# Gate and up tiles of three feed-forward layers from seven quarter products

## Chip, cores and metric

One core of a Trainium2 chip runs the whole program. The metric is device microseconds of one execution; the kernel before has a median of 2692.7 us over three runs (2689.73 to 2694.28). TensorE (PE) multiplies; VectorE (DVE), ScalarE (ACT) and GpSimd (POOL) do the rest, each taking its instructions in a fixed order; SyncE (SP) issues the DMAs. TensorE's clock has two levels, 1.2 and 2.4 GHz; the granted clock is given as a share of the upper one.

## The reference

Eight stages over a sequence of 512 positions with 1024 features: four mixers (two attentions, a state-space layer, a convolution), and after each a feed-forward layer of the same form:

```python
def swiglu_ffn(u, w_gate, w_up, w_down):       # u: 512 x 1024 (normed), F = 2816
    return (jax.nn.silu(u @ w_gate) * (u @ w_up)) @ w_down
x = x + swiglu_ffn(rmsnorm(x, g), w_gate, w_up, w_down)
```

All of it is fp32.

## The kernel before

Activations lie transposed: 8 chunks of 128 features x 512 positions. Each fp32 operand is split into two fp32r tiles, `hi` (a cast on ACT) and `lo` = value - `hi` (a subtraction on DVE; `split`, L293 and L294, for weights), and each product is three matmuls, hi x hi, hi x lo, lo x hi (`mm3`, L301 to L303), all accumulated in PSUM.

A feed-forward layer has 22 hidden tiles of 128 features. `gu` (L685) makes one tile j: it loads gate and up weights (two DMAs of 512 KB into the three `raw` buffers), splits them into the four `hi`/`lo` buffers of `wspl`, and runs 8 chunks x 2 x 3 = 48 matmuls of 512 columns, gate into PSUM tile `pg`, up into `pu`. Then silu(gate) x up goes into `s` (a name for the pool `z`, which has three buffers), and `hilo_of` splits it into a pair of `d` tiles. `dn` (L711) makes one of 8 output chunks from a range of hidden tiles and adds it to `xT` (L670, L674). The hidden tiles are taken in three parts (`PARTS`: 8, 7 and 7 tiles); after each part come 8 `dn` items over it.

Layers 0 and 1 come behind a `Split` norm, whose input h is already normed; their first `gu` takes tiles 0 and 1 together. Layers 2 and 3 come behind a `Norm`: h is only gained, and the row factor R (column sums on PE, an inverse square root of 13 small DVE instructions, a transpose on PE into `rb`, a copy on ACT) multiplies gate and up later (L704, L706). R is asked for once the first tile's matmuls are written.

The program is written tile by tile; a scheduler then fixes the order of each engine from its own timing of the program, and a buffer's next user waits until the last reader of it is done. `phase` opens the pools of a stage.

Of the kernel before, what the change touches and what calls it, by code (L numbers as in the profile page):

```python
# [10 lines left out]
F32 = mybir.dt.float32  # L11
F32R = mybir.dt.float32r
I32 = mybir.dt.int32
AF = mybir.ActivationFunctionType
OP = mybir.AluOpType
PSUM = bass.MemoryType.PSUM

T, NT, KC = 512, 4, 8
PARTS = ((0, 8), (8, 15), (15, 22))
F_HID, FC = 2816, 22  # L20
NEG = -1e30

# [66 lines left out]
def _layout(i):  # L89
# [20 lines left out]
    for n in range(4):  # L110
# [44 lines left out]
    "ssm": (SSB,  # L155
# [63 lines left out]
def _program(nc, tc, a, out, stages=STAGES):  # L219
    st = ExitStack()  # L220
    pool = lambda n, b, **k: st.enter_context(tc.tile_pool(name=n, bufs=b, **k))
    one = pool("one", 1)
    wraw = pool("wraw", 3)
# [3 lines left out]
    cur = {"sb": None, "ps": None}  # L227

    def phase(name, kinds=("sb", "ps")):
        for k in kinds:  # L230
            if cur[k]:
                cur[k][0].close()
            e = ExitStack()
            kw = {"space": PSUM} if k == "ps" else {}
            p = e.enter_context(tc.tile_pool(name=f"{k}_{name}", bufs=1, reuse_waits="tile", **kw))
            cur[k] = (e, p, PHASES[name][k == "ps"])

    def ptile(k, shape, dt, name):
        tag = ALIAS.get(name, name)
        _, p, bufs = cur[k]  # L240
        if k == "ps" and tag not in bufs:
            tag = {"tr": "pt", "st": "tr", "py": "tr"}[tag]
        return p.tile(shape, dt, tag=tag, name=name, bufs=bufs[tag])


    V, S, E, G = nc.vector, nc.scalar, nc.tensor, nc.gpsimd
# [27 lines left out]
    def tmp(name="t", dt=F32, n=T):  # L274
        return ptile("sb", [128, n], dt, name)
# [4 lines left out]
    def psum(name="ps"):  # L280
        return ptile("ps", [128, T], F32, name)

    last_load = [None]
# [6 lines left out]
    def split(raw, n, m=128, eng=None):  # L290
        hi = wspl.tile([128, n], F32R, tag="hi", name="hi")
        lo = wspl.tile([128, n], F32R, tag="lo", name="lo")
        S.copy(hi, raw)  # L293
        (eng or V).tensor_tensor(lo, raw, hi.bitcast(F32), op=OP.subtract)  # L294
        return hi.rearrange("p (k m) -> p k m", m=m), lo.rearrange("p (k m) -> p k m", m=m)

    def two(src):
        return [split(load(flat(src[:, i]), 1024), 1024) for i in range(2)]

    def mm3(ps, lh, ll, rh, rl, start, stop, **k):  # L300
        E.matmul(ps, lh, rh, start=start, stop=False, **k)  # L301
        E.matmul(ps, lh, rl, start=False, stop=False, **k)  # L302
        E.matmul(ps, ll, rh, start=False, stop=stop, **k)  # L303
# [7 lines left out]
    def flat(ap):  # L311
        return ap.rearrange("p k m -> p (k m)")
# [60 lines left out]
    def hilo_of(src, bias=None, gain=None, to="h"):  # L373
        if to == "h":
            hi, lo = (hp.tile([128, T], F32R, tag="h", name=n) for n in ("hi", "lo"))
        else:
            hi, lo = tmp(to, F32R), tmp(to, F32R)
        if gain is not None:
            S.activation(hi, src, AF.Copy, scale=gain)
            V.scalar_tensor_tensor(lo, src, gain, hi.bitcast(F32), op0=OP.mult, op1=OP.subtract)  # L380
        elif bias is not None:
            S.activation(hi, src, AF.Identity, bias=bias)
            V.scalar_tensor_tensor(lo, src, bias, hi.bitcast(F32), op0=OP.add, op1=OP.subtract)
        else:
            S.copy(hi, src)  # L385
            V.tensor_tensor(lo, src, hi.bitcast(F32), op=OP.subtract)
        return hi, lo
# [279 lines left out]
    def add_x(m, ps, gcol, bias=None, o=slice(0, T)):  # L667
# [5 lines left out]
        else:  # L673
            V.tensor_tensor(x, ps, x, op=OP.add)  # L674

    def ffn(n, nm, gcol, nxt):
        phase("ffn")
        direct = isinstance(nm, Split)
        h = nm.h
        d = {}  # L680

        def gu(js):
            def it():
                gr = []
                for j in js:  # L685
                    with tc.issue_after(nm.mark.ins) if direct and j == 1 else nullcontext():
                        W = direct and j == 0 and nm.W or two(a[f"w_gu{n}"][j])
                        gr += [(psum("pg"), W[0]), (psum("pu"), W[1])]
                if js[0] == 0 and direct:
                    nm.lin([gr[:2], gr[2:]])  # L690
                else:
                    lin(gr, h)
                if nm.R is None:
                    nm.finish().to_sbuf()
                R = nm.R
                for i, j in enumerate(js):
                    pg, pu = gr[2 * i][0], gr[2 * i + 1][0]
                    s = tmp("s")
                    if direct:
                        S.activation(s, pg, AF.Silu)  # L700
                        V.tensor_tensor(s, s, pu, op=OP.mult)
                    else:
                        u = tmp("su")
                        V.tensor_tensor(s, pg, R, op=OP.mult)  # L704
                        S.activation(s, s, AF.Silu)
                        V.tensor_tensor(u, pu, R, op=OP.mult)  # L706
                        V.tensor_tensor(s, s, u, op=OP.mult)
                    d[j] = hilo_of(s, to="d")
                return 10.4 * len(js), None
            return it  # L710

        def dn(m, lo, hi):
            def ev(ps):
                add_x(m, ps, gcol)
                return nxt.update(m) if nxt and hi == FC else None
            return item(a[f"w_dn{n}"][m][:, lo:hi], lambda: [d[j] for j in range(lo, hi)], ev, hi - lo)

        items = []
        for lo, hi in PARTS:
            if lo == 0 and direct:  # L720
                items += [gu([0, 1])] + [gu([j]) for j in range(2, hi)]
            else:
                items += [gu([j]) for j in range(lo, hi)]
            at = TAIL_AT["final" if isinstance(nxt, Final) else 7]
            n_tail = at[0] if hi == FC and isinstance(nxt, Split) else 0
            items += [dn(m, lo, hi) for m in range(KC - n_tail)]
            if n_tail:
                items.append(tail(range(KC - n_tail, KC), lambda m: a[f"w_dn{n}"][m][:, lo:hi], hi - lo,
                                  lambda: [d[j] for j in range(lo, hi)], gcol, nxt, ("pj",) * n_tail, at[1:]))
        return _stream(items)  # L730
# [939 lines left out]
    nm = None  # L1670
    if stages[0] != "mix0":
# [7 lines left out]
        nm = norms[stages[0]]().all()  # L1679
    for i, name in enumerate(stages):  # L1680
# [14 lines left out]
        else:  # L1695
            n = int(name[3])
            f = ffn(n, nm, (None, md0.col(40), md1.col(40))[n + 1] if n < 2 else None, nx)
# [5 lines left out]
        nm = nx  # L1703
# [19 lines left out]
```

## Time and profile before

| | |
|---|---|
| median of 3 runs | 2692.7 us |
| the profiled execution, its span | 2689.29 us, 2687.5 us |
| PE busy | 2554.3 us (95%) |
| DVE, ACT, POOL busy | 1611.3, 1056.1, 396.3 us |
| mean granted TensorE clock | 0.979 |

Busy time of PE counts any time in which a matmul is in flight, so PE at 100% says that it never waited, not that it ran at its peak. How long one matmul takes from the next is read from the start times in the timeline, not from durations, which overlap. In the timelines DVE instructions overlap too: a duration is longer than the distance to the next start.

### The profile page before, as it was taken

Reading aid. Unit: us, or ns where it says so; the run is one execution under the profiler, and the core shown is the slowest. Engines: PE = TensorE matmul, PEld = TensorE weight load, DVE = VectorE, ACT = ScalarE, POOL = GpSimd, SP = SyncE. Lnnn points to the kernel's source line nnn. Section 1 sums busy time; section 2 is a strip of 40 time slices with the busy share of each in tenths; the row PEclk is TensorE's granted clock in tenths of the full one; section 3 lists DMA queues with packets and bytes.
Section 4 is the critical chain, followed back from the end, with each engine's and each line's share of the span. In section 5 each row is a group of like instructions: output and inputs, shape, how many; then the busy total and the mean of one; then the engine's idle time right before and its main releaser. Section 6 shows DMA issues by size and latency. Waiting matters only on the chain.

```text
span 2687.5 us, 33768 instructions
## 1 busy us (share of the span) xinstructions
PE 2554.3 (95%) x13016; PEld 2155.4 (80%) x13016; DVE 1611.3 (60%) x2898; ACT 1056.1 (39%) x1881; POOL 396.3 (15%) x286
## 2 busy tenths in 40 slices
PE   5788989999999999999999999999999997999998
PEld 4666888888888888888788888788888877888887
DVE  8898765555457643333678786643444897543444
ACT  4457643222357542222455444422223554422222
POOL 3345120000113210000100000100001783100001
PEclk9988999999999999999999999999999997999999
DMA  7711135555421123333222122233323220332332
GB/s 270 230 53 40 32 101 198 176 174 187 144 81 32 48 88 101 91 97 95 87 79 72 55 79 59 91 104 100 94 94 95 64 63 16 100 103 95 94 97 69
DMA packets 81251, 265.40 MB, mean 99 GB/s; under 512 B 8897, under 2 KB 11329, under 8 KB 81089
## 3 DMA queue, kind: packets, MB, share of 16 engines
q1 hardware_dynamic: 81088, 263.24, 31.1%
q8 instruction: 102, 1.67, 0.3%
q14 instruction: 61, 0.49, 0.1%
HBM read 261.10 MB, written 2.10 MB: 98 GB/s over the span
## 4 chain that ended last, share of the span: by engine, by line
PE 79%; DVE 11%; POOL 3%; ACT 3%; issue 2%; DMA 2%; SPq 0%; POOLq 0%; DVEq 0%; ACTq 0%
PE pj L301 10%; PE pj L303 10%; PE pj L302 10%; PE pg L301 6%; PE pg L303 6%; PE pg L302 6%; PE pu L301 6%; PE pu L303 6%; PE pu L302 6%; POOL yp L1490 2%; DMA araw<-ada 1%; PE pj L1302 1%; PE pj L1303 1%; PE pj L1304 1%; DVE lo L294 1%
## 5 line engine op out<-in xcount | busy, mean ns | idle before, releaser
L293 ACT CAST hi<-raw 128x1024 fp32r<-128x1024 f32 (+4 forms) x421 | 412.3, 993 | 1047.8 <-PE pg L302 541.6
L294 DVE TENSOR_TENSOR lo<-raw,hi 128x1024 fp32r<-128x1024 f32 (+3 forms) x411 | 483.0, 1187 | 259.4 <-ACT hi L293 254.3
L301 PE MATMUL pj<-d,hi 128*128 128x512 f32 (+1 forms) x952 | 360.2, 382 | 2.1 <-ACT d L385 1.0
L303 PE MATMUL pj<-d,lo 128*128 128x512 f32 (+1 forms) x952 | 358.5, 377 | 0.0
L302 PE MATMUL pj<-d,hi 128*128 128x512 f32 (+1 forms) x952 | 355.8, 374 | 0.0
L301 PE MATMUL pg<-hi 128*128 128x512 f32 (+1 forms) x808 | 308.8, 382 | 5.0 <-DVE z L476 4.4
L303 PE MATMUL pg<-hi,lo 128*128 128x512 f32 (+1 forms) x808 | 307.9, 381 | 2.1 <-DVE lo L294 2.1
L302 PE MATMUL pg<-lo,hi 128*128 128x512 f32 (+1 forms) x808 | 307.9, 381 | 0.6 <-DVE lo L487 0.6
L301 PE MATMUL pu<-hi 128*128 128x512 f32 (+1 forms) x736 | 280.5, 381 | 3.2 <-DVE z L476 3.2
L302 PE MATMUL pu<-lo,hi 128*128 128x512 f32 (+1 forms) x736 | 280.1, 381 | 0.0
L303 PE MATMUL pu<-hi,lo 128*128 128x512 f32 (+1 forms) x736 | 280.1, 381 | 0.0
L440 POOL TENSOR_TENSOR acc<-acc,sq 128x256 f32<-128x256 f32 (+1 forms) x49 | 52.3, 1069 | 1123.9 <-ACT sq L438 799.2
L302 PE MATMUL pj<-lo,hi 128*128 128x512 f32 (+2 forms) x520 | 206.9, 398 | 3.3 <-DVE lo L487 2.4
L301 PE MATMUL pj<-hi 128*128 128x512 f32 (+2 forms) x520 | 206.7, 401 | 3.0 <-ACT qk L791 1.2
L303 PEld LDWEIGHTS pj<-d,lo 128*128 128x128 f32 x952 | 179.2, 188 | 35.0 <-issue 0.5
L301 PEld LDWEIGHTS pj<-d,hi 128*128 128x128 f32 x952 | 178.8, 189 | 34.8 <-issue 1.5
L302 PEld LDWEIGHTS pj<-d,hi 128*128 128x128 f32 x952 | 179.3, 188 | 33.9 <-issue 1.0
L303 PE MATMUL pj<-hi,lo 128*128 128x512 f32 (+2 forms) x520 | 204.5, 394 | 0.3 <-DVE lo L294 0.3
L301 PEld LDWEIGHTS pg<-hi 128*128 128x128 f32 x808 | 153.1, 190 | 33.7 <-issue 5.6
L303 PEld LDWEIGHTS pg<-hi,lo 128*128 128x128 f32 x808 | 153.4, 190 | 31.3 <-DVE lo L294 2.6
L302 PEld LDWEIGHTS pg<-lo,hi 128*128 128x128 f32 x808 | 153.6, 190 | 29.1 <-DVE lo L487 0.8
L704 DVE TENSOR_TENSOR s<-pg,R 128x512 f32<-128x512 f32 x44 | 30.4, 691 | 234.9 <-PE pg L303 222.3
(434 smaller groups left out, 4623.6 us busy)
## 6 DMA issues: line engine op xcount, KB each, us to landing
raw<-w_gu SPq DMA_DIRECT2D x176, 512.0 KB, 4.0
araw<-ada SPq DMA_DIRECT2D x96, 512.0 KB, 6.0
raw<-w_dn SPq DMA_DIRECT2D x64, 448.0 KB, 3.9
raw<-w_dn SPq DMA_DIRECT2D x32, 512.0 KB, 4.0
raw<-w_p SPq DMA_DIRECT2D x24, 512.0 KB, 3.7
raw<-w_out SPq DMA_DIRECT2D x32, 256.0 KB, 3.1
raw<-w_xs SPq DMA_DIRECT2D x16, 512.0 KB, 3.6
raw<-w_z SPq DMA_DIRECT2D x16, 512.0 KB, 3.6
```

What stands on the lines that cost most here:

```text
L293: S.copy(hi, raw)
L294: (eng or V).tensor_tensor(lo, raw, hi.bitcast(F32), op=OP.subtract)
L301: E.matmul(ps, lh, rh, start=start, stop=False, **k)
L302: E.matmul(ps, lh, rl, start=False, stop=False, **k)
L303: E.matmul(ps, ll, rh, start=False, stop=stop, **k)
L440: G.tensor_tensor(self.acc[:, o], self.acc[:, o], sq[:, o], op=OP.add)
L704: V.tensor_tensor(s, pg, R, op=OP.mult)
L1302: E.matmul(o, xh[:, ts], wh[:, k], start=st_, stop=False, skip_group_check=True)
L1303: E.matmul(o, xh[:, ts], wl[:, k], start=False, stop=False, skip_group_check=True)
L1304: E.matmul(o, xl[:, ts], wh[:, k], start=False, stop=sp, skip_group_check=True)
L1490: G.tensor_tensor(yp[:, sft:], yp[:, sft:], pr[:, sft:], op=OP.add)
```

## The change

Layer 0 stays as it was. In layers 1, 2 and 3 the first tiles (three in layer 1, one in layers 2 and 3) stay as they were; each of the other 19 + 21 + 21 = 61 tiles is made by `gu7`. It takes gate and up weights, each in a lower and an upper half of the features, and the activations in four quarters (lower or upper half of the features, first or second half of the positions) as a 2x2 by 2x2 block product, which Strassen's scheme (in Winograd's form) makes of seven quarter products: each 4 chunks x 3 matmuls of 256 columns, 84 matmuls in all. `seven` forms the weight sums s1 to s4 on DVE, splits 3.5 tiles of 1024 columns instead of 2, and lets the products accumulate in three PSUM regions r1, r2, r3, with four copies of partial sums to SBUF on ACT (`ua`, `bu`) between the products of r1 and r3. Gate is then y + ua on DVE, and the two halves of up lie in r1 and in `bu` (one POOL addition).

`crossed` runs once a layer, ahead of the first `gu7`: for each of four pairs of chunks, two POOL additions join `hi` and `lo` again (into `z`), four half-width DVE instructions make the four combinations of quarters, an ACT cast and a DVE subtraction split them (`xh`, `xl`). The hidden tiles of these layers go in four parts (6, 6, 5, 5) and have 12 `d` buffers instead of 16. A `hi`/`lo` buffer of `wspl` is used once per tile by each of its four splits.

```diff
@@ -17,6 +17,8 @@
 
 T, NT, KC = 512, 4, 8
 PARTS = ((0, 8), (8, 15), (15, 22))
+PARTS_S = ((0, 6), (6, 12), (12, 17), (17, 22))
+FIRST_S = (22, 3, 1, 1)
 F_HID, FC = 2816, 22
 NEG = -1e30
 
@@ -151,7 +153,8 @@
              {"mm": 2, "lg": 3, "tr": 2, "py": 1}),
     "mix1": ({"wb": 3, "d": 26, "wd": 1, "z": 4, "zt": 3, "yn": 5, "sq": 3, "re": 3},
              {"mm": 2, "lg": 2, "tr": 2, "py": 1, "st": 1}),
-    "ffn": ({"araw": 6, "cb": 2, "d": 16, "z": 3, "su": 2, "sq": 2}, {"mm": 6, "st": 1, "tr": 1}),
+    "ffn0": ({"araw": 6, "cb": 2, "d": 16, "z": 3, "su": 2, "sq": 2}, {"mm": 6, "st": 1, "tr": 1}),
+    "ffn": ({"d": 12, "z": 3, "su": 2, "sq": 2, "ws": 3, "xh": 4, "xl": 4, "ua": 2, "bu": 2}, {"mm": 6, "st": 1, "tr": 1}),
     "ssm": (SSB,
             {"mm": 2, "lg": 2, "tr": 2, "py": 1, "st": 1}),
     "conv": ({"dwh": 1, "dwl": 1, "dgh": 2, "dgl": 2, "d": 8, "sg": 3, "cv": 8, "yp": 2, "pr": 3, "z": 3, "sq": 2},
@@ -673,8 +676,79 @@
         else:
             V.tensor_tensor(x, ps, x, op=OP.add)
 
+    def crossed(h):
+
+
+        out = []
+        hv = T // 2
+        for k in range(4):
+            z1, z2 = tmp("z"), tmp("z")
+            for z, c in ((z1, k), (z2, k + 4)):
+                G.tensor_tensor(z, h[c][0].bitcast(F32), h[c][1].bitcast(F32), op=OP.add)
+            t = wide1("ws")
+            q = [t[:, i * hv:(i + 1) * hv] for i in range(4)]
+            V.tensor_tensor(q[0], z1[:, :hv], z1[:, hv:], op=OP.subtract)
+            V.scalar_tensor_tensor(q[1], z2[:, hv:], -1.0, q[0], op0=OP.mult, op1=OP.subtract)
+            V.tensor_tensor(q[2], z2[:, hv:], z1[:, hv:], op=OP.subtract)
+            V.scalar_tensor_tensor(q[3], q[1], -1.0, z2[:, :hv], op0=OP.mult, op1=OP.subtract)
+            hi, lo = wide1("xh", F32R), wide1("xl", F32R)
+            S.copy(hi, t)
+            V.tensor_tensor(lo, t, hi.bitcast(F32), op=OP.subtract)
+            out.append([(hi[:, i * hv:(i + 1) * hv], lo[:, i * hv:(i + 1) * hv]) for i in range(4)])
+        return out
+
+    def wide1(tag, dt=F32):
+        _, p, bufs = cur["sb"]
+        return p.tile([128, 1024], dt, tag=tag, name=tag, bufs=bufs[tag])
+
+    def seven(g, u, h, x4):
+
+
+        hv = T // 2
+        wa, wd = (wraw.tile([128, 1024], F32, tag="raw", name="raw") for _ in range(2))
+        wb, wc = wide1("ws"), wide1("ws")
+        g1, s1, s2, s4, s3, g2, u1, u2 = [w[:, o:o + 512] for w in (wa, wb, wc, wd) for o in (0, 512)]
+        for t, src in ((g1, g[:, :4]), (wd, u), (g2, g[:, 4:])):
+            last_load[0] = nc.sync.dma_start(t, flat(src))
+        V.tensor_tensor(s1, u1, u2, op=OP.add)
+        ah, al = split(wa, 1024)
+        V.tensor_tensor(s2, s1, g1, op=OP.add)
+        V.tensor_tensor(s4, s2, g2, op=OP.add)
+        bh, bl = split(wb, 1024)
+        V.tensor_tensor(s3, g1, u1, op=OP.add)
+        ch, cl = split(wc, 1024)
+        uh, ul = split(u2, 512)
+        x, y = psum("pg"), psum("pu")
+        r1, r2, r3 = x[:, :hv], y[:, :hv], y[:, hv:]
+        ua, bu = tmp("ua"), tmp("bu")
+        one_, two_ = slice(0, hv), slice(hv, T)
+        quarter = lambda c, t: [(h[c + k][0][:, t], h[c + k][1][:, t]) for k in range(4)]
+        cross = lambda i: [x4[k][i] for k in range(4)]
+
+        def product(r, wh, wl, o, xs, start):
+            for k in range(4):
+                mm3(r, wh[:, o + k], wl[:, o + k], xs[k][0], xs[k][1], start and k == 0, False, skip_group_check=True)
+
+        product(r1, ah, al, 0, quarter(0, one_), True)
+        S.copy(ua[:, :hv], r1)
+        product(r3, ah, al, 4, cross(0), True)
+        S.copy(bu[:, :hv], r3)
+        product(r1, bh, bl, 0, cross(1), False)
+        S.copy(ua[:, hv:], r1)
+        product(r3, bh, bl, 4, quarter(4, two_), False)
+        product(r1, ch, cl, 0, cross(2), False)
+        S.copy(bu[:, hv:], r1)
+        product(r2, ch, cl, 4, quarter(4, one_), False)
+        product(r1, uh, ul, 0, cross(3), False)
+        s = tmp("s")
+        V.tensor_tensor(s, y, ua, op=OP.add)
+        G.tensor_tensor(bu[:, :hv], bu[:, :hv], bu[:, hv:], op=OP.add)
+        return s, r1, bu[:, :hv]
+
     def ffn(n, nm, gcol, nxt):
-        phase("ffn")
+        sparse = FIRST_S[n] < FC
+        phase("ffn" if sparse else "ffn0")
+        x4 = []
         direct = isinstance(nm, Split)
         h = nm.h
         d = {}
@@ -709,6 +783,27 @@
                 return 10.4 * len(js), None
             return it
 
+        def gu7(j):
+            def it():
+                if not x4:
+                    x4.extend(crossed(h))
+                hv = T // 2
+                g, u = (a[f"w_gu{n}"][j][:, i] for i in range(2))
+                s, u0, u1 = seven(g, u, h, x4)
+                if direct:
+                    S.activation(s, s, AF.Silu)
+                else:
+                    if nm.R is None:
+                        nm.finish().to_sbuf()
+                    V.tensor_tensor(s, s, nm.R, op=OP.mult)
+                    S.activation(s, s, AF.Silu)
+                    V.tensor_tensor(s, s, nm.R, op=OP.mult)
+                for o, v in ((slice(0, hv), u0), (slice(hv, T), u1)):
+                    V.scalar_tensor_tensor(s[:, o], s[:, o], -1.0, v, op0=OP.mult, op1=OP.mult)
+                d[j] = hilo_of(s, to="d")
+                return 10.4, None
+            return it
+
         def dn(m, lo, hi):
             def ev(ps):
                 add_x(m, ps, gcol)
@@ -716,11 +811,12 @@
             return item(a[f"w_dn{n}"][m][:, lo:hi], lambda: [d[j] for j in range(lo, hi)], ev, hi - lo)
 
         items = []
-        for lo, hi in PARTS:
+        for lo, hi in (PARTS_S if sparse else PARTS):
+            b = lo
             if lo == 0 and direct:
-                items += [gu([0, 1])] + [gu([j]) for j in range(2, hi)]
-            else:
-                items += [gu([j]) for j in range(lo, hi)]
+                items.append(gu([0, 1]))
+                b = 2
+            items += [gu([j]) if j < FIRST_S[n] else gu7(j) for j in range(b, hi)]
             at = TAIL_AT["final" if isinstance(nxt, Final) else 7]
             n_tail = at[0] if hi == FC and isinstance(nxt, Split) else 0
             items += [dn(m, lo, hi) for m in range(KC - n_tail)]
```

The order of the instructions at three places. First PE in layer 2, where the first tile ends and the second starts; before, around the transpose `rb` that spreads R (`pg`, `pu` are the PSUM tiles of gate and up):

```order
L301 MATMUL pu<-hi 128x512
L302 MATMUL pu<-lo,hi 128x512
L303 MATMUL pu<-hi,lo 128x512
L370 MATMUL rb<-cst,rstd 128x128 x4
L301 MATMUL pg<-hi 128x512
L302 MATMUL pg<-lo,hi 128x512
```

Now (`ss` is the PSUM tile of the column sums, `xh` and `xl` are the crossed quarters):

```order
L367 MATMUL ss<-ones,sq 128x1 x4
L304 MATMUL pg<-hi 128x256
L305 MATMUL pg<-lo,hi 128x256
L306 MATMUL pg<-hi,lo 128x256
...
L373 MATMUL rb<-cst,rstd 128x128 x4
L304 MATMUL pu<-xh,hi 128x256
L305 MATMUL pu<-xl,hi 128x256
L306 MATMUL pu<-xh,lo 128x256
```

Before, `rb` stands behind the 48 matmuls of the second tile and in front of the third's. Now only the first quarter product (12 matmuls on h alone) stands between the column sums and `rb`, and the second quarter product, which reads `xh` and `xl`, follows at once.

DVE at the same place, before, from the end of the inverse square root:

```order
L358 SCALAR_TENSOR_TENSOR rstd<-rt,rstd 128x4
L704 TENSOR_TENSOR s<-pg,R 128x512
L706 TENSOR_TENSOR su<-pu,R 128x512
L704 TENSOR_TENSOR s<-pg,R 128x512
L707 TENSOR_TENSOR s<-s,su 128x512
L706 TENSOR_TENSOR su<-pu,R 128x512
L294 TENSOR_TENSOR lo<-raw,hi 128x1024 x2
```

And now:

```order
L361 SCALAR_TENSOR_TENSOR rstd<-rt,rstd 128x4
L778 TENSOR_TENSOR s<-pg,R 128x512
L780 TENSOR_TENSOR su<-pu,R 128x512
L690 TENSOR_TENSOR ws<-z 128x256
L781 TENSOR_TENSOR s<-s,su 128x512
L691 SCALAR_TENSOR_TENSOR ws<-z,ws 128x256
L692 TENSOR_TENSOR ws<-z 128x256
L693 SCALAR_TENSOR_TENSOR ws<-ws,z 128x256
L389 TENSOR_TENSOR d<-s,d 128x512
L690 TENSOR_TENSOR ws<-z 128x256
L696 TENSOR_TENSOR xl<-ws,xh 128x1024
L691 SCALAR_TENSOR_TENSOR ws<-z,ws 128x256
```

The crossing (L690 to L696, four rounds) stands behind the instruction that waits for R.

DVE over one tile in the middle of layer 3, before:

```order
L704 TENSOR_TENSOR s<-pg,R 128x512
L706 TENSOR_TENSOR su<-pu,R 128x512
L294 TENSOR_TENSOR lo<-raw,hi 128x1024 x2
L707 TENSOR_TENSOR s<-s,su 128x512
L386 TENSOR_TENSOR d<-s,d 128x512
```

And now, a stretch that is 12 of the 14 instructions of a tile:

```order
L744 TENSOR_TENSOR s<-pu,ua 128x512
L389 TENSOR_TENSOR d<-s,d 128x512
L798 TENSOR_TENSOR s<-s,R 128x512
L297 TENSOR_TENSOR lo<-ws,hi 128x1024
L713 TENSOR_TENSOR raw<-raw 128x512
L718 TENSOR_TENSOR ws<-raw 128x512
L800 TENSOR_TENSOR s<-s,R 128x512
L297 TENSOR_TENSOR lo<-raw,hi 128x512
L715 TENSOR_TENSOR ws<-raw 128x512
L297 TENSOR_TENSOR lo<-raw,hi 128x1024
L802 SCALAR_TENSOR_TENSOR s<-s,pg 128x256
L802 SCALAR_TENSOR_TENSOR s<-s,bu 128x256
```

Six DVE instructions a tile have become fourteen.

## Rows read from the trace of the kernel before

**Rows 1.** The page: busy time by engine, and the chain that ended last.

```profile
PE 2554.3 (95%) x13016; PEld 2155.4 (80%) x13016; DVE 1611.3 (60%) x2898; ACT 1056.1 (39%) x1881; POOL 396.3 (15%) x286
...
PE 79%; DVE 11%; POOL 3%; ACT 3%; issue 2%; DMA 2%; SPq 0%; POOLq 0%; DVEq 0%; ACTq 0%
```

**Rows 2.** Windows, layer 3: length, busy PE, PEld, DVE, ACT, POOL, clock, DMA.

```profile
2450.00:2470.00 20.00, 20.00 (x90) 16.57 (x89) 8.42 (x10) 5.68 (x7) 0.00 (x0) 1.00 0.19 61
```

**Rows 3.** DVE timeline, one tile of layer 3: start, duration, line, operands, [idle before].

```profile
2455.64 0.69 DVE L704 TENSOR_TENSOR s<-pg,R 128x512 f32<-128x512 f32 x1 [8.17 <-PE pg L303]
2456.31 0.69 DVE L706 TENSOR_TENSOR su<-pu,R 128x512 f32<-128x512 f32 x1
2456.92 2.35 DVE L294 TENSOR_TENSOR lo<-raw,hi 128x1024 fp32r<-128x1024 f32 x2
2459.19 0.69 DVE L707 TENSOR_TENSOR s<-s,su 128x512 f32<-128x512 f32 x1
2460.56 0.69 DVE L386 TENSOR_TENSOR d<-s,d 128x512 fp32r<-128x512 f32 x1 [0.69 <-ACT d L385]
2466.51 0.69 DVE L704 TENSOR_TENSOR s<-pg,R 128x512 f32<-128x512 f32 x1 [5.26 <-PE pg L303]
```

**Rows 4.** PE timeline, 256-column matmuls, one PSUM region at a time, layer 2's end.

```profile
2072.42 0.28 PE L301 MATMUL pj<-d,hi 128*128 128x256 f32 x1
...
2078.66 0.28 PE L303 MATMUL pj<-d,lo 128*128 128x256 f32 x1
```

**Rows 5.** PE timeline, 256-column matmuls of the state-space stage.

```profile
1351.83 0.28 PE L1304 MATMUL pj<-hi,lo 128*128 128x256 f32 x1
...
1355.91 0.28 PE L1303 MATMUL pj<-lo,hi 128*128 128x256 f32 x1
```

**Rows 6.** PE timeline, layer 2: column sums behind the first tile, and `rb`.

```profile
1730.24 0.95 PE L364 MATMUL ss<-ones,acc 128*128 128x1 f32 x8
...
1731.94 0.49 PE L301 MATMUL pg<-hi 128*128 128x512 f32 x1
...
1740.24 0.60 PE L370 MATMUL rb<-cst,rstd 128*128 128x128 f32 x4
```

**Rows 7.** DVE timeline, layer 2: first and last instruction of the inverse square root.

```profile
1732.89 0.15 DVE L341 TENSOR_SCALAR rm<-ss 128x4 f32<-128x4 f32 x1
...
1735.06 0.16 DVE L358 SCALAR_TENSOR_TENSOR rstd<-rt,rstd 128x4 f32<-128x4 f32 x1
```

**Rows 8.** ACT timeline, layer 2: the copy of R, and what follows.

```profile
1740.88 0.58 ACT L423 COPY R<-rb 128x512 f32<-128x512 f32 x1 [9.36 <-PE rb L370]
1741.48 1.28 ACT L705 ACT_TABLE_LOAD   x1
```

**Rows 9.** DVE timeline, convolution: 256-column instructions back to back.

```profile
2263.73 0.41 DVE L1609 TENSOR_TENSOR cv<-cv,mub 128x256 f32<-128x256 f32 x1
2264.06 0.41 DVE L1608 TENSOR_TENSOR cv<-cv,mub 128x256 f32<-128x256 f32 x1
```

**Rows 10.** POOL timeline, behind the convolution.

```profile
2291.38 5.74 POOL L403 TENSOR_TENSOR acc<-acc,sq 128x512 f32<-128x512 f32 x3 [46.19 <-ACT sq L399]
2299.73 1.41 POOL L403 TENSOR_TENSOR acc<-acc,sq 128x512 f32<-128x512 f32 x1 [2.61 <-ACT sq L399]
```

**Rows 11.** DVE timeline of the same stretch.

```profile
2292.28 2.31 DVE L294 TENSOR_TENSOR lo<-raw,hi 128x1024 fp32r<-128x1024 f32 x1
2295.97 2.23 DVE L294 TENSOR_TENSOR lo<-raw,hi 128x1024 fp32r<-128x1024 f32 x1 [1.38 <-ACT hi L293]
...
2298.78 1.21 DVE L294 TENSOR_TENSOR lo<-raw,hi 128x1024 fp32r<-128x1024 f32 x1
```

**Rows 12.** Windows, end of the convolution (columns as in rows 2).

```profile
2242.00:2247.00 5.00, 1.87 (x8) 1.78 (x8) 4.96 (x7) 0.17 (x1) 3.19 (x3) 0.50 0.00 0
...
2257.00:2262.00 5.00, 5.00 (x35) 5.00 (x35) 3.00 (x8) 2.35 (x5) 0.00 (x0) 0.75 0.01 2
```

**Rows 13.** PE's waits: who for whom, us in total, times, longest.

```profile
PE ss L457 <- POOL acc L440: 6.3, 4, 2.9
```

## The prediction

> **What bounds the kernel now.** I read the page first: PE is busy 95% of the span, and 79% of the chain that ended last is PE [rows 1]. Then the windows of a gate and up stretch: PE 20.00 of 20 us at clock 1.00, DVE 8.42, ACT 5.68, POOL nothing [rows 2]. So there PE is the bound, and the three others have room. Then the timelines, for the price of one step. The s of one tile follows that of the last by 2466.51 - 2455.64 = 10.87 us [rows 3]; over 48 matmuls that is 0.2265 us each. A matmul of 256 columns is no half of that: 53 steps from 2072.42 to 2078.66 give 0.1177 us [rows 4], 34 steps from 1351.83 to 1355.91 give 0.1200 [rows 5]. Each carries some 10 to 13 ns that don't shrink with its columns.
>
> **The matmuls.** A tile has 84 x 0.1177 = 9.89 us instead of 10.87. I take the first price, since a quarter product, like the matmuls of rows 4, stays in one PSUM region for its whole run; those of rows 5 are the upper price (10.08). That is 0.98 us a tile (0.79), and over 61 tiles **59.8 us gained** (48.2). Seven for eight would be one eighth, 1.36 us a tile; the 36 additional matmuls eat a quarter of that. The down products keep their number of matmuls, and their columns.
>
> The Trainium skill (TensorE: Matmul & The Clock Gate, section "Wait — 56ns, not 53.3ns?") gives a warm matmul columns / 2.4 GHz plus 2.5 ns: an estimate of 109.2 ns here and 215.8 ns before. By it the tile would gain 48 x 0.2158 - 84 x 0.1092 = 1.19 us, 72 us in all, and my sum below would end 12 us earlier. Rows 3 to 5 show more at both widths, and the measurement decides.
>
> **The crossing.** This is the large cost. The second quarter product of the first `gu7` tile reads the crossed quarters, and PE takes its queue in order, so nothing behind it can run. I count from E, the end of the last matmul written in the old manner.
>
> In layers 2 and 3, DVE's next instruction behind the square root is s = pg x R, and the whole crossing stands behind it. Before, R had the 48 matmuls of the second tile to hide under. Now it comes at E + 1.70 (column sums, 1730.24 to 1731.94, [rows 6]) + 2.33 (square root, 1732.89 to 1735.22, [rows 7]) + 0.60 (`rb`, [rows 6]) + 0.58 (copy of R, [rows 8]) and some 0.3 of handing over: E + 5.5.
>
> From there to the last `xl`, on which the second product ends, DVE has 27 instructions: 4 of 1024 columns at 1.13 (half of 2459.19 - 2456.92), 7 of 512 columns at 0.61 to 0.67 [rows 3], 16 of 256 columns at 0.33 (2264.06 - 2263.73, [rows 9]): 4.5 + 4.5 + 5.3 = 14.4 us with the dependent ones at full length. Waiting for silu behind a table load (1.28, [rows 8]) adds 0.6, and the last two matmuls 0.25: the second product ends at E + 20.7. Without a wait it would end at E + 1.70 + 1.41 + 0.4 + 1.41 = E + 4.9. So PE stands still for **15.8 us at least**.
>
> On top of this come POOL's additions. Two of the eight are done before E. Since `z` has three buffers, which `s` shares, the other six wait until DVE has read an earlier pair, and each pair's combinations wait for them. What an addition costs beside DVE, the rows behind the convolution show: while POOL ran three additions, the same DVE subtraction took 2.31 and 2.23 us, and 1.21 us when POOL stood still [rows 10, 11]. The two take turns. At 1.41 us an addition [rows 10] the six add up to 8.5 us, 24.3 us in all. The Trainium skill (SBUF — State Buffer, section "SBUF: two separate sides") states the rule: a DVE instruction with two SBUF inputs and a GpSimd one that reads SBUF lock the same port pair, and the loser waits for the whole instruction. The trace agrees (2.23 against 1.21). If they didn't exclude each other, the hand-made sequence of the round trips would end at 18.9 instead.
>
> In layer 1 nothing waits for R: DVE resumes 0.9 us after E, with one multiplication less; 13.9 us of list, 0.6 of waits and 0.25 end at E + 15.7, where E + 2.8 is due: 12.8 at least, 21.3 with the additions. The three layers: 44.4 at least, 69.9 at most. I take **63 us lost**, near the upper end, to which the rows are nearest, less 2.3 a layer for additions that run in DVE's own waits.
>
> A thin stretch of PE also costs clock: the granted clock was 0.50 (1.2 GHz) where PE was busy 1.87 of 5 us, and still 0.75 on average over the next stretch that PE filled [rows 12]. A quarter of 5 us, three times: **4 us** (0 to 8).
>
> **DVE over a tile.** Layers 2 and 3: 3 x 1.13 (lo of 1024) + 9 x 0.64 (four sums, y + ua, twice R, two lo of 512) + 2 x 0.35 = 9.85 us, by the prices of rows 3 and 9. One POOL addition of half width locks it out for another 0.7 (half of 1.41): 10.5 us, where PE needs 9.89. Before, it was 8.42 of 20 us [rows 2]. So DVE becomes the bound here by some 0.65 us a tile. It is softened: `hi` and `lo` of the next tile are ready about 2 us early, and in the down stretches DVE catches up. A part of 5.5 tiles lags 3.6 us, less 2.1 of lead, 1.5 us a part; eight parts 12 us, and the first part of each layer, which starts without a lead, 2 more each: **16 us lost** (0 with more lead; 27 with none, 40 if each tile also has 0.3 of waits of its own). Layer 1 has no R, 1.3 us less: 9.2, below PE.
>
> Costs at nothing, and their cover: the four copies of partial sums a tile on ACT stand two quarter products (2.8 us) ahead of the product that needs them, because the scheduler puts the last product of a tile behind the first two of the next; uncovered, each would be 0.4 us and 61 x 4 of them 98 us. The `hi` casts (ACT some 6 us a tile of 9.9). The loads move the same bytes. The eight additional down items a layer keep their matmuls; their evacuations stay under PE. At the ends of layers 2 and 3 the last part has 5 tiles instead of 7, so fewer matmuls cover the chain from sums of squares to the norm's first tile; PE waits 6.3 us there in all now [rows 13], and I add half: **3 us** (0 to 6).
>
> **The sum.** - 59.8 + 63 + 4 + 16 + 3 = + 26 us on the profiled execution of 2689.3, which is 3.4 us under the median: 2719 us against 2692.7.
>
> **Rivals.**
> *DVE bound throughout.* If DVE's in-order queue loses half a microsecond a tile in waits for ACT's casts (it has fourteen instructions, six of which wait for another engine), a tile of layers 2 and 3 takes 11.0 us, no less than the 10.87 of before. Then only layer 1 gains, 18.6 us: - 18.6 + 5 + 63 + 4 + 3 = + 56, 2749 us. For it: 10.5 of a 9.89 us tile. Against it: the down stretches and the leads.
> *Faster.* POOL's additions fall wholly into DVE's waits, so that each crossing costs its DVE list alone (44.4 in all), and the leads take up DVE's excess. Then - 59.8 + 44.4 + 2 = - 13, 2679 us. It decides when the three gaps together stay under 50 us and the tiles keep 9.9 us. For it: PE's gain is certain and all else is hidden. Against it: rows 10 and 11.
> *It cancels.* Gaps of some 50 us and a DVE excess of 6: 2693 us. That the change doesn't do what it says is not among the cases: the order has 84 matmuls a tile.
>
> **How the numbers follow.** Forecast 0.50, DVE bound throughout 0.26, faster 0.15, cancels 0.09. A measurement of this kernel can tell about 0.2%, 5.4 us, from no change. Faster 0.15, same 0.09, slower 0.76. The unknown costs reach from - 59.8 + 44.4 = - 15 to - 48.2 + 69.9 + 8 + 40 + 6 = + 76; I leave out the last 8 us above, where every term stands at its worst: 2678 to 2760. The forecast's own range, with the steady excess between 5 and 27 and the gaps between 53 and 70, is 2698 to 2738.
>
> **What the profile of the changed kernel would show.** One gap on PE in each of layers 1 to 3, in front of the second quarter product, waiting for DVE's `xl`: some 19, 22 and 22 us; a granted clock below 1 behind it. DVE and POOL in turns in it, POOL's additions at 1.4 us or more. Half-width matmuls 0.118 to 0.120 us apart. Tiles of layer 1 9.9 to 10.1 us apart, of layers 2 and 3 10.1 to 10.6, with waits of PE for DVE's `lo`. DVE over 85% busy in these stretches. I am wrong if the gaps sum up to less than 45 us or to more than 75, if PE waits for ACT's copies, or if a tile of layers 2 and 3 takes over 10.8 us.

## The result and the profile after

The changed kernel takes 2717.1 us (median of 4 runs, 2713.7 to 2719.5) against 2693.5 of the kernel before: 1.0087 of its time, 95% interval 1.0069 to 1.0106. Forecast was 2719. The profiled execution, its span 2717.7 us, is 30.2 us above that of before; 5.4 of these lie ahead of layer 1, where the two programs are alike. The rest is read in three stretches, each from the first gate matmul of a layer to that of the next (or to the end), by PE's timeline. Here and below (each ratio further down is to the kernel before as measured beside that run, 2692.5 to 2695.6 us):

| kernel (profiled execution) | layer 1 to 2 | layer 2 to 3 | layer 3 to the end | median, us |
|---|---|---|---|---|
| before | 779.1 | 592.6 | 375.6 | 2693.5 |
| changed | 787.8 | 601.2 | 383.1 | 2717.1 |
| `no_crossing` | 772.3 | 582.9 | 366.0 | 2667.2 |
| `z_own` | 786.1 | 596.1 | 379.4 | 2704.8 |
| `z_dve` | 785.1 | 600.2 | 381.9 | 2713.1 |
| `early` | 777.7 | 593.2 | 379.6 | 2695.2 |
| `ahead` | 774.7 | 575.8 | 362.8 | 2662.8 |
| `ahead2` | 778.6 | 583.6 | 370.8 | 2679.4 |
| `four_parts` | 779.2 | 590.4 | 377.1 | 2692.9 |
| `dve_more` | 792.9 | 606.0 | 389.2 | 2735.0 |
| `best_halves` | 770.4 | 576.6 | 361.2 | 2652.6 |
| `best_whole` | 765.4 | 576.1 | 361.1 | 2653.1 |
| `best_tail` | 766.3 | 577.2 | 358.6 | 2646.4 |

The change lost 8.7 + 8.6 + 7.5 = 24.8 us in the three. The page first, as [rows 1]:

```profile
PE 2525.8 (93%) x15176; PEld 2229.9 (82%) x15176; DVE 1987.6 (73%) x3494; ACT 1250.1 (46%) x2283; POOL 534.6 (20%) x371
...
PE 75%; DVE 13%; issue 3%; POOL 3%; DMA 3%; ACT 3%; POOLq 0%; SPq 0%; DVEq 0%; ACTq 0%
```

A steady stretch of layer 3 (a window, columns as in [rows 2]; then the first and last of 492 matmuls on PE's timeline):

```profile
2460.00:2510.00 50.00, 50.00 (x423) 50.00 (x423) 46.57 (x66) 30.30 (x50) 11.76 (x5) 1.00 0.30 99
```

```profile
2454.95 0.28 PE L304 MATMUL pg<-hi 128*128 128x256 f32 x1
...
2513.30 0.28 PE L306 MATMUL pg<-xh,lo 128*128 128x256 f32 x1
```

58.35 / 491 = 0.1188 us a matmul, 9.98 a tile instead of 10.87. PE never waits here, though DVE works 46.57 of 50 us. The steps aren't all alike: behind a matmul that reads crossed quarters (`xh`, `xl`) the next one starts after 0.118 us on average, behind one that reads h after 0.120, in layers 1 to 3 alike.

What PE waits for is the crossing, for its casts as much as for its subtractions (waits of the whole program; then PE's timeline in layer 3, from the column sums to the end of the second quarter product):

```profile
PE pu L304 <- ACT xh L695: 23.7, 12, 5.4
PE pu L305 <- DVE xl L696: 21.8, 9, 3.6
```

```profile
2345.51 0.95 PE L367 MATMUL ss<-ones,acc 128*128 128x1 f32 x8
...
2349.78 0.65 PE L373 MATMUL rb<-cst,rstd 128*128 128x128 f32 x4 [0.89 <-DVE rstd L361]
2355.45 0.58 PE L304 MATMUL pu<-xh,hi 128*128 128x256 f32 x1 [5.01 <-ACT xh L695]
2359.65 0.58 PE L305 MATMUL pu<-xl,hi 128*128 128x256 f32 x1 [3.62 <-DVE xl L696]
...
2372.63 0.41 PE L306 MATMUL pu<-xh,lo 128*128 128x256 f32 x1
```

The product ends at 2372.84, 27.3 us after E (2345.51), where E + 4.9 would do: 22.4 us. DVE and POOL in the meantime:

```profile
2351.09 0.69 DVE L778 TENSOR_TENSOR s<-pg,R 128x512 f32<-128x512 f32 x1 [1.36 <-ACT R L426]
...
2355.91 1.48 DVE L690 TENSOR_TENSOR ws<-z 128x256 f32<-128x256 f32 x1
2357.31 2.28 DVE L696 TENSOR_TENSOR xl<-ws,xh 128x1024 fp32r<-128x1024 f32 x1
...
2370.61 1.22 DVE L696 TENSOR_TENSOR xl<-ws,xh 128x1024 fp32r<-128x1024 f32 x1
```

```profile
2354.12 4.39 POOL L687 TENSOR_TENSOR z<-hi,lo 128x512 f32<-128x512 f32 x3 [15.87 <-DVE ws L692]
2360.41 2.72 POOL L687 TENSOR_TENSOR z<-hi,lo 128x512 f32<-128x512 f32 x2 [1.89 <-DVE ws L692]
```

R comes at E + 5.6 as worked out from [rows 6 to 8]. Beside POOL's additions the same instructions take 1.48 instead of 0.41 and 2.28 instead of 1.21, as in [rows 11]. The rule of the Trainium skill (SBUF — State Buffer, section "SBUF: two separate sides"), that the two exclude each other, agrees. The clock, as in [rows 12]:

```profile
2345.00:2350.00 5.00, 4.11 (x33) 3.79 (x33) 1.99 (x13) 0.37 (x1) 0.00 (x0) 1.00 0.00 0
2350.00:2355.00 5.00, 0.43 (x4) 0.19 (x2) 3.91 (x8) 2.49 (x4) 0.88 (x1) 0.86 0.00 0
2355.00:2360.00 5.00, 0.94 (x2) 0.64 (x3) 5.00 (x5) 0.39 (x1) 3.51 (x3) 0.50 0.00 0
...
2370.00:2375.00 5.00, 3.72 (x14) 3.13 (x15) 4.95 (x6) 4.28 (x6) 0.00 (x0) 0.50 0.42 157
2375.00:2380.00 5.00, 5.00 (x35) 5.00 (x35) 3.81 (x6) 1.42 (x2) 0.00 (x0) 0.75 0.51 162
```

Once the product can run, PE is at 1.2 GHz for some 4.5 us more (about 2 us lost).

How large a crossing is in all: from the first gate matmul to the second part's takes 124.0, 120.8 and 120.3 us in the three layers. `four_parts`, with the same parts of tiles in the old manner, takes 106.0, 100.7 and 100.6; three or five tiles at 0.89 less make 103.4, 96.2 and 96.1. The crossings cost 20.6 + 24.6 + 24.2 = 69.4 us, clock included.

### The profile page after: what moved, and what is told of

The parts are those of the page before. It is cut to its first block, busy times and chain, and to the rows that moved or that the text cites. A ratio compares the mean times of both kernels' runs of the same rounds, so it can differ in the third digit from the quotient of the medians.

```text
span 2717.7 us, 39747 instructions
## 1 busy us (share of the span) xinstructions
PE 2525.8 (93%) x15176; PEld 2229.9 (82%) x15176; DVE 1987.6 (73%) x3494; ACT 1250.1 (46%) x2283; POOL 534.6 (20%) x371
## 4 chain that ended last, share of the span: by engine, by line
PE 75%; DVE 13%; issue 3%; POOL 3%; DMA 3%; ACT 3%; POOLq 0%; SPq 0%; DVEq 0%; ACTq 0%
PE pj L304 10%; PE pj L306 10%; PE pj L305 10%; PE pg L304 6%; PE pg L306 6%; PE pg L305 6%; PE pu L306 5%; PE pu L304 5%; PE pu L305 5%; POOL yp L1586 2%; DVE lo L297 2%; DMA araw<-ada 1%; PE pj L1398 1%; PE pj L1399 1%; PE pj L1400 1%
## 5 line engine op out<-in xcount | busy, mean ns | idle before, releaser
L296 ACT CAST hi<-raw 128x1024 fp32r<-128x1024 f32 (+5 forms) x445 | 392.9, 891 | 721.2 <-PE pj L305 262.4
L297 DVE TENSOR_TENSOR lo<-raw,hi 128x1024 fp32r<-128x1024 f32 (+5 forms) x435 | 462.2, 1068 | 146.8 <-ACT hi L296 144.3
L304 PE MATMUL pu<-hi 128*128 128x256 f32 (+1 forms) x736 | 229.9, 312 | 3.3 <-DVE z L479 3.2
L306 PE MATMUL pu<-hi,lo 128*128 128x256 f32 (+1 forms) x736 | 229.5, 312 | 0.0
L305 PE MATMUL pu<-lo,hi 128*128 128x256 f32 (+1 forms) x736 | 229.4, 312 | 0.0
L304 PE MATMUL pg<-xh,hi 128*128 128x256 f32 x732 | 206.8, 283 | 2.2 <-ACT hi L296 2.2
L306 PE MATMUL pg<-xh,lo 128*128 128x256 f32 x732 | 206.5, 282 | 0.1
L305 PE MATMUL pg<-xl,hi 128*128 128x256 f32 x732 | 205.8, 281 | 0.0
L304 PE MATMUL pg<-hi 128*128 128x256 f32 (+1 forms) x564 | 188.3, 334 | 5.5 <-DVE z L479 4.4
L306 PE MATMUL pg<-hi,lo 128*128 128x256 f32 (+1 forms) x564 | 187.3, 332 | 2.2 <-DVE lo L297 2.2
```

## The experiments

**Without the crossing** (`no_crossing`).

```diff
-                    x4.extend(crossed(h))
+                    hq = T // 2
+                    x4.extend([[(h[k][0][:, o], h[k][1][:, o]) for o in (slice(0, hq), slice(hq, T))] * 2 for k in range(4)])
```

> The changed kernel without its three crossings: the quarter products that read crossed quarters read plain quarters of the activations instead, so the sums are other numbers, with the same matmuls. Theory: the three gaps of PE that the changed kernel shows ahead of its second quarter product (about 21, 25 and 24 us) are the crossing and nothing else, so about 70 us go: 2717 - 70 = 2647 us (2640 to 2655). Rival: part of each gap is the wait for the row factor R and for the first weight sums, which stay; then 10 to 15 us of each gap stay and the time is 2675 to 2695.

2667.2 us, 0.9904 (0.9888 to 0.9921): 50 us less, not 70. Yet the gaps are gone: the first parts take 104.3, 100.2 and 100.1 us, 60.5 less in all, and behind the first 9 us of a layer (in layer 1 the norm is still at work in them) no two matmuls of them start more than 1.2 us apart. The rest of the program gave 9.7 us back: the seven-product tiles and the down matmuls of layers 1 to 3 are slower, at the same granted clock. Windows of a gate and up stretch and of a down stretch of layer 1, here:

```profile
1060.00:1100.00 40.00, 40.00 (x335) 40.00 (x335) 34.55 (x46) 23.65 (x41) 4.63 (x4) 1.00 0.34 106
...
1021.00:1046.00 25.00, 25.00 (x109) 20.26 (x108) 15.68 (x22) 7.17 (x9) 0.00 (x0) 1.00 0.34 106
```

and in the changed kernel:

```profile
1080.00:1120.00 40.00, 40.00 (x340) 40.00 (x339) 34.76 (x48) 24.08 (x40) 3.42 (x4) 1.00 0.33 107
...
1043.00:1068.00 25.00, 25.00 (x111) 20.51 (x110) 16.02 (x22) 7.46 (x9) 0.00 (x0) 1.00 0.33 106
```

1.5 and 1.8% fewer matmuls in the same time. In the gate and up stretch every matmul now reads h, and every step is 0.120 us, the price of h in the changed kernel too; that covers most of the 1.5%. The down steps are 0.2333 us instead of 0.2289. The numbers in the operands are no sufficient explanation: half of the first down stretch of layer 1 reads hidden tiles 0 to 2, made in the old manner from unchanged numbers, and not one of its steps is under 0.233 us. And the gate and up matmuls of the plain tiles aren't slower, though in layers 2 and 3 their numbers are others; nor are the down stretches of layer 0 (43.7 us for the first, as before). What makes the others slower, no run shows. So the total understates the crossing, and the first parts are the better measure. The rival (10 to 15 us a gap stay) falls: in layers 2 and 3 three waits of 0.6 to 0.8 us stay.

**The additions' buffers** (`z_own`) **and their engine** (`z_dve`).

```diff
-            z1, z2 = tmp("z"), tmp("z")
+            z1, z2 = tmp("d"), tmp("d")
```

> The eight sums hi + lo of a crossing are written into free d buffers instead of the three z buffers, so that POOL's additions no longer wait until DVE has read an earlier pair; nothing else changes. Theory of the prediction (the additions add about 8.5 us to each gap because they run between DVE's instructions and the two engines take turns): they now run ahead of DVE's list, the gaps fall by about 8 us each, 2717 - 24 = 2693 us. Rival (DVE's list alone sets the gap, POOL's additions are covered by it): no change, 2717.

```diff
-                G.tensor_tensor(z, h[c][0].bitcast(F32), h[c][1].bitcast(F32), op=OP.add)
+                V.tensor_tensor(z, h[c][0].bitcast(F32), h[c][1].bitcast(F32), op=OP.add)
```

> The eight sums hi + lo of a crossing are made on DVE instead of POOL, in the same three buffers. Theory (an addition on POOL costs DVE's list as much as it takes on POOL): DVE's list gets 8 x 0.61 = 4.9 us longer and loses 8.5 of turns, so each gap falls by 3.6 us, 2717 - 11 = 2706 us. Rival (POOL's additions are covered): the gaps grow by 4.9 us each, 2732.

`z_own`: 2704.8 us, 1.0049 (1.0030 to 1.0068), half of the expected gain. In layer 3 POOL's additions are done before DVE begins (POOL, then DVE):

```profile
2327.69 10.12 POOL L687 TENSOR_TENSOR d<-hi,lo 128x512 f32<-128x512 f32 x7 [1.96 <-DVE lo L383]
```

```profile
2341.82 0.69 DVE L778 TENSOR_TENSOR s<-pg,R 128x512 f32<-128x512 f32 x1 [1.36 <-ACT R L426]
...
2347.93 1.23 DVE L696 TENSOR_TENSOR xl<-ws,xh 128x1024 fp32r<-128x1024 f32 x1 [0.77 <-ACT xh L695]
...
2357.63 1.23 DVE L696 TENSOR_TENSOR xl<-ws,xh 128x1024 fp32r<-128x1024 f32 x1 [0.51 <-ACT xh L695]
```

From s to the end of the last `xl` DVE now takes 17.0 us instead of 20.7. The first parts are 3.3, 4.0 and 3.7 us shorter: that is what it is worth to have the additions out of the way, not 8.5. DVE's own list with its waits for the casts is 17.0, not 15. `z_dve`: 2713.1 us, 1.0077 (1.0060 to 1.0093); the first parts are 3.6, 1.9 and 1.2 us shorter. Its interval overlaps that of the changed kernel, so a gain is not shown; the theory's 2706 us (1.0050) lies below the interval, and the rival's 2732 far above it.

**The crossing beside plain tiles**, in two halves behind the first items (`early`), or whole and ahead of R (`ahead`, `ahead2`).

```diff
-FIRST_S = (22, 3, 1, 1)
+FIRST_S = (22, 4, 3, 3)
@@ gu, at the item's end
+                if sparse and len(x4) < 4:
+                    x4.extend(crossed(h, (len(x4), len(x4) + 1)))
```

> The crossing is written in two halves behind the first and the second plain item of a layer, and one plain tile more in layer 1 and two more in layers 2 and 3 stand between it and the first tile of seven products. Theory (the crossing is 70 us of DVE and POOL work with nothing for PE to do beside it; the steady tiles are PE's): it runs beside the plain tiles, and what is left is 5 tiles x 0.9 us less gain: 2647 + 4.5 = 2652 us, up to 2662 with a few us of wait left in each layer. Rival (DVE has no room for it: the crossing then delays the weight sums and the lo splits of the first seven-product tile, and the gap only moves): 2680 to 2700.

2695.2 us, 1.0010 (0.9999 to 1.0022): the rival's number, but by another mechanism. DVE had room and didn't use it; layer 2, DVE and POOL:

```profile
1744.18 0.69 DVE L778 TENSOR_TENSOR s<-pg,R 128x512 f32<-128x512 f32 x1 [5.54 <-ACT R L426]
```

```profile
1749.26 3.05 POOL L687 TENSOR_TENSOR z<-hi,lo 128x512 f32<-128x512 f32 x2 [21.92 <-DVE ws L692]
```

The crossing was still queued behind R, which now stands behind the second tile's matmuls, and POOL waited 21.9 us for a buffer. Hence:

```diff
+            z1, z2 = tmp("d"), tmp("d")
@@ gu, behind lin(gr, h) and ahead of nm.finish()
+                if sparse and not x4:
+                    x4.extend(crossed(h, range(4)))
```

> The whole crossing is written ahead of the row factor R (right behind the matmuls of the first plain item), its sums go to free d buffers, and one plain tile more in layer 1 and two more in layers 2 and 3 stand in front of the first tile of seven products. Theory (in the run with the crossing in two halves DVE stood idle for 5.5 us until R came, with the crossing queued behind it, and the additions then waited for buffers; both go): the first part of a layer takes 105 to 108 us instead of 124, 120.8 and 120.3, so 2717 - 17 - 2 x 14 = about 2670 us. Rival (DVE has no room beside the plain tiles; what is written ahead of R delays R, the evacuations and the weight sums by the same time): 2690 to 2700, as with the two halves.

> As the run before it, with the plain tiles of the changed kernel in layer 1 (three) and two instead of three in layers 2 and 3. Theory (17 us of crossing fit under one and a half plain tiles of 10.9 us each, less 4 us a tile of DVE's other work): 3 tiles x 0.9 us gained, 2 to 6 us of wait a layer given back; 2670 to 2680. Rival (two plain tiles cover it wholly): 2667.

(`ahead` keeps the FIRST_S of `early`; `ahead2` has (22, 3, 2, 2).) `ahead`: 2662.8 us, 0.9895 (0.9878 to 0.9913). `ahead2`: 2679.4 us, 0.9953 (0.9940 to 0.9966), with 3.9 us between the starts of two matmuls in the second product of layers 2 and 3; some 10 us a layer stay there, where the theory had 2 to 6, and the time is at the upper end of its range. In `ahead` these layers are clear: their first parts take 98.3 and 98.2 us, where `four_parts` less three tiles at 0.89 gives 98.0 and 97.9: next to nothing of the gaps is left. Layer 1 kept 114.1, 10 too many (ACT's timeline, then PE's):

```profile
977.77 1.04 ACT L695 CAST xh<-ws 128x1024 fp32r<-128x1024 f32 x1 [6.88 <-DVE ws L693]
978.72 1.04 ACT L296 CAST hi<-raw 128x1024 fp32r<-128x1024 f32 x1
```

```profile
979.82 0.80 PE L304 MATMUL pg<-hi 128*128 128x512 f32 x1 [4.24 <-ACT hi L296]
...
982.66 0.80 PE L304 MATMUL pu<-hi 128*128 128x512 f32 x1 [1.62 <-ACT hi L296]
```

The `hi` cast of the third tile stood in ACT's queue behind an `xh` that waited 6.9 us for DVE, which was taking turns with POOL.

**Parts alone** (`four_parts`: FIRST_S all 22, four parts in layers 1 to 3) **and more work for DVE** (`dve_more`).

> The kernel before with one part of the change alone: layers 1 to 3 in four parts of 6, 6, 5 and 5 tiles with 12 d buffers, every tile made in the old manner. Theory (the last part has 5 down matmul triples an item instead of 7, so less stands in front of the next stage's statistics; the changed kernel lost some 10 us between the layers): 5 to 10 us slower than before, 2698 to 2703. Rival (the loss between the layers comes from the seven-product tiles): no change, 2693.

2692.9 us, 0.9997 (0.9988 to 1.0006): the four parts cost nothing in all by themselves. At the program's end they do cost something: from the last down matmul to the end it is 11.6 us before and 12.9 here (12.9 in the changed kernel too).

```diff
         V.tensor_tensor(s3, g1, u1, op=OP.add)
+        V.tensor_tensor(s3, g1, u1, op=OP.add)
+        V.tensor_tensor(s3, g1, u1, op=OP.add)
```

> The changed kernel with the sum s3 of every seven-product tile made three times instead of once: two more DVE instructions of 512 columns, 1.2 us a tile. Theory of the trace after (DVE works 9.35 of 9.97 us a tile in layers 2 and 3 and is just not the bound): DVE needs 10.55 us a tile there and sets the pace, up to 42 x 0.58 = 24 us more, some of it taken up in the down stretches; 2725 to 2741. Layer 1 has 1.2 us less on DVE and doesn't change. Rival (the leads of hi and lo take it up): 2717 to 2720.

2735.0 us, 1.0160 (1.0146 to 1.0173), 18 more. Here PE does wait in the steady stretch (x412 where x423 were):

```profile
2467.00:2517.00 50.00, 49.18 (x412) 48.61 (x410) 46.28 (x67) 26.70 (x45) 10.39 (x4) 1.00 0.31 98
```

The second and third parts of layers 2 and 3 are 6.5 us longer together, so DVE has less than 1.2 us a tile to spare there. But the three first parts, where the additional sums stand in the crossing's queue, are 8.7 us longer: the total came out as expected, more than half of it from the gap and not from the steady tiles. Layer 1 lost 5.1 us too, against the expectation, 3.6 of them in its first part.

**Layer 1 mended.** The crossing of layer 1 in two halves behind its first two items (`best_halves`) or whole behind the second (`best_whole`), with five plain tiles; and the first of these with parts of 5, 5, 5 and 7 tiles (`best_tail`). Layers 2 and 3 are as in `ahead`.

```diff
-FIRST_S = (22, 4, 3, 3)
+FIRST_S = (22, 5, 3, 3)
@@ best_tail
-PARTS_S = ((0, 6), (6, 12), (12, 17), (17, 22))
+PARTS_S = ((0, 5), (5, 10), (10, 15), (15, 22))
```

> Layers 2 and 3 as in the run with the crossing ahead of R. In layer 1 the crossing is written in two halves behind the first and the second plain item, with five plain tiles instead of four. Theory (in the run ahead of R, layer 1 still had 10 us too much, because its crossing ran in front of the third tile's lo splits and beside POOL's additions, and PE waited for those splits): the lo splits come first, the 10 us go, one tile gives back 0.9: 2663 - 9 = 2654 us. Rival (layer 1 has no place for the crossing, and the wait only moves to the first seven-product tile): 2660 to 2665.

> As the run before it, with the whole crossing of layer 1 behind its second plain item. Theory (17 us of DVE list under two plain tiles of 10.9 us that need 4 us of DVE each): 2654 to 2657. Rival (too late by a few microseconds, as where it was in the changed kernel): 2658 to 2662.

> As the run with two halves in layer 1, with the hidden tiles in parts of 5, 5, 5 and 7 instead of 6, 6, 5 and 5, and 14 d buffers. Theory of the prediction (a last part of 5 tiles covers less of the chain to the next norm): some 3 to 6 us faster than the run with halves. Rival (the four-part run showed no loss, so the parts don't matter): within 2 us of it.

2652.6 us (0.9846, 0.9824 to 0.9868), 2653.1 (0.9847, 0.9826 to 0.9868) and **2646.4 us (0.9824, 0.9804 to 0.9844)**: the last beats the kernel before by 47 us and the changed one by 71. The halves left no wait over 1 us in layer 1 behind its first 9 us. With the longer last part the median is 6 us lower, as expected, but the intervals overlap, and the profiles don't carry that size: from layer 1 on, `best_tail` is 6.1 us shorter than `best_halves` and only 0.6 shorter than `best_whole`, which has the short last part as well (why, below). What the longer part is worth isn't settled by these runs. Layer 2 of `best_tail`, where the crossing was a gap:

```profile
1735.00:1745.00 10.00, 10.00 (x49) 8.40 (x48) 10.00 (x16) 6.97 (x10) 0.00 (x0) 1.00 0.28 93
1745.00:1755.00 10.00, 10.00 (x84) 9.84 (x84) 9.91 (x15) 5.50 (x11) 0.93 (x1) 1.00 0.34 97
```

## Why the prediction was right, and where not

The time, the sign and the cause (the crossing, in front of PE's in-order queue) held. Of the signs that the prediction named, the gaps (20.6, 24.6 and 24.2 us), the half-width step and the tiles of layer 1 came; the tiles of layers 2 and 3 at 10.1 us or more, with waits for `lo`, did not. Of the terms:

| term | predicted | measured |
|---|---|---|
| 61 tiles of 84 matmuls | -59.8 (-48.2) | -54.3 (61 x 0.89) |
| crossings with their clock | +63 and +4 | +69.4 |
| DVE as bound in layers 2 and 3 | +16 | 0 |
| between the layers | +3 | +9.7 (the rest of 24.8) |
| sum | +26 | +24.8 |

*The matmuls.* 0.1188 us lies between the two prices, 0.1177 [rows 4] and 0.1200 [rows 5]; one PSUM region at a time was no reason for the lower: products into the same region have both, by what they read (0.118 over crossed quarters, four of the seven; 0.120 over h). The estimate of 109.2 ns worked out from the Trainium skill (TensorE: Matmul & The Clock Gate, section "Wait — 56ns, not 53.3ns?") is not what the trace shows.

*The crossing* was right in sum and in its steps up to R. In the gap of layer 3 the six additions take 8.4 us on POOL, and six DVE instructions beside them are longer by 0.9 to 1.1 us each, 6.2 in all: the 8.5 less 2.3 of the prediction. What it had wrong is what this is worth. Without the additions DVE's list takes 17.0 us instead of 15 (`z_own`), since waits for casts come up that the turns with POOL had covered; so they add only 3.7. The 18.9 that the prediction gives for engines that don't exclude each other has no working there, and no run shows it.

*DVE over a tile* is the step that failed: 16 us for a bound that isn't there. The second and third parts of a layer take 92.8 and 77.3 us in layer 1 and in layers 2 and 3 alike. I charged 0.64 us for each 512-column instruction and 0.7 for POOL's addition, 10.5 in all. Back to back the instructions start 0.60 apart. As to the addition, a DVE instruction beside it is longer in 28 of the 61 cases, by 0.4 to 0.6 us, which is 0.24 a tile instead of 0.7; otherwise it is POOL that stands back, or the two don't meet (an addition takes 1.67 us on average and 0.74 alone). The page of the changed kernel; then one of DVE's weight sums, alone and beside an addition; then that addition:

```profile
L745 POOL TENSOR_TENSOR bu<-bu 128x256 f32<-128x256 f32 x61 | 102.0, 1672 | 807.5 <-ACT bu L740 594.3
```

```profile
2485.97 0.67 DVE L713 TENSOR_TENSOR raw<-raw 128x512 f32<-128x512 f32 x1
...
2495.26 1.23 DVE L713 TENSOR_TENSOR raw<-raw 128x512 f32<-128x512 f32 x1
```

```profile
2494.98 0.96 POOL L745 TENSOR_TENSOR bu<-bu 128x256 f32<-128x256 f32 x1 [4.19 <-ACT bu L740]
```

46.57 of 50 us is 9.30 a tile, 0.68 under PE's 9.98. `dve_more` shows how near the rival "DVE bound throughout" was: with 1.2 us more a tile on DVE, a part of it comes true (a second part of six tiles in layers 2 and 3 takes 2.2 to 2.5 us more).

*Between the layers* I gave a reason (the shorter last part) and a third of the size, and read [rows 13] wrongly: of those 6.3 us, 2.4 lie ahead of layer 0, 0.5 behind it and 2.9 ahead of layer 1, and only 0.5 at the end of layer 2. By itself the reason is worth the 1.3 us at the program's end that `four_parts` shows. Of the 9.7 us, 5.0 lie between the last down matmul of layer 1 and the first gate matmul of layer 2 (416.2 us, in `four_parts` 411.2). There PE waits twice for the last chunk's `lo` and `hi`, and behind that the clock falls:

```profile
1322.21 0.50 PE L305 MATMUL pj<-lo,hi 128*128 128x512 f32 x1 [0.87 <-DVE lo L383]
...
1324.87 0.50 PE L304 MATMUL pj<-hi 128*128 128x512 f32 x1 [0.89 <-ACT hi L382]
```

```profile
1325.00:1330.00 5.00, 4.83 (x20) 3.58 (x21) 3.09 (x12) 1.04 (x1) 0.00 (x0) 0.62 0.39 122
1330.00:1335.00 5.00, 5.00 (x17) 2.12 (x16) 0.81 (x5) 0.00 (x0) 0.00 (x0) 0.69 0.23 91
```

The clock doesn't fall every time. In `ahead` PE has the same two waits, and the granted clock stays at 1.00:

```profile
1310.80 0.50 PE L305 MATMUL pj<-lo,hi 128*128 128x512 f32 x1 [0.91 <-DVE lo L383]
...
1313.45 0.50 PE L304 MATMUL pj<-hi 128*128 128x512 f32 x1 [0.89 <-ACT hi L382]
```

```profile
1314.00:1319.00 5.00, 4.83 (x27) 3.04 (x27) 3.02 (x14) 1.04 (x1) 0.00 (x0) 1.00 0.48 150
1319.00:1324.00 5.00, 4.06 (x21) 2.37 (x19) 2.05 (x5) 2.00 (x3) 0.00 (x0) 1.00 0.15 60
```

There the way to layer 2 takes 413.5 us: some 2.3 of the 5.0 come with the waits and some 2.7 with the clock, by these two executions. It fell in `best_halves` (416.7) and not in `best_whole` (412.9), each with the 0.89 us wait alone; that is most of what sets `best_tail` (412.4) apart from `best_halves`. With a last part of 7 tiles neither wait is there, as in `four_parts`, and from layer 3 to the end `best_tail` takes 2.5 us less than both of the others. So a short last part costs the waits only where its tiles are made of seven products; why, stays open, and so does the rest of the 9.7 us.

So two errors of opposite sign, 16 too much and 6.7 too little, with 5.5 too much gain and 2.4 too little crossing, brought the sum within 2 us; that closeness is partly luck. The profiled execution of the changed kernel is also the slowest of its four.

## What to carry to other kernels

A scheme that saves an eighth of the products per tile (here 0.89 of 10.87 us) has a price that is paid once a layer; here the place of that work in the queues decided the sign, not its size: 69 us of crossing became about 2 (`best_halves`) once DVE had it ahead of what it waits for, its sums had free buffers, and PE had three to five plain tiles to work on (0.89 us of gain forgone for each). When writing work earlier, look at each engine's queue: the same move that cleared layers 2 and 3 put a waiting cast in front of layer 1's weights. Price back-to-back instructions by the distance of their starts, and ask of two engines that exclude each other which one has waits to spare. Before a small loss is put down to an edit, see whether the granted clock fell in one profile and not in the other.

## What was not expected of the hardware

In the changed kernel the step between 256-column matmuls is 0.118 us where they read crossed quarters and 0.120 where they read h, at a granted clock of 1.00. In `no_crossing` the down matmuls of layers 1 to 3 took 0.2333 us instead of 0.2289 at that clock, those over unchanged numbers too; the cause is open. Two waits of PE under 1 us behind layer 1 were followed by two stretches of 5 us at a granted clock of 0.62 and 0.69 in the changed kernel, and by none in `ahead`.
